# Trips of turned results and probabilities through DRAM: begun by GpSimd instead of SyncE

## The chip, the cores and the metric

The kernel runs on one core of one Trainium2 chip. The metric is device time in microseconds (us), here the median of three runs. The core has five engines with a queue of instructions each: TensorE (PE, with its weight loads as PEld) multiplies matrices, VectorE (DVE) and ScalarE (ACT) work on tiles, GpSimd (POOL) does a few elementwise operations here, and SyncE (SP) only begins DMAs. Each queue is worked off in the order in which the program was written, and an instruction that waits holds all that stand behind it on its engine.

## The reference

One layer of a hybrid encoder, in float32, on 256 tokens of 2048 features:

```python
u   = rmsnorm(h, g_mix)
b_a, c_a, v_a, q, k, v, gl_a, gl_b = split(u @ w_in)
y_a = (b_a * dwconv3(c_a * v_a, conv_w)) @ w_out_a
att = banded_window_attention(rope(q), rope(k), v, sink)      # 16 heads of 64, 4 kv heads
y_b = att @ w_o_attn
h   = h + (sigmoid(gl_a + b) * y_a + sigmoid(gl_b + b) * y_b) @ w_mix_out
up  = dwconv3(rmsnorm(h, g_ffn) @ ffn_w_up) + bias            # 2 x 5632 columns
h   = h + (silu(up[:5632]) * up[5632:]) @ ffn_w_down
out = rmsnorm(h, g_final)
```

## The kernel before, in words

Activations lie transposed on the chip: features on the 128 partitions, the 256 tokens along the row. Every weight is streamed from DRAM once, in chunks of 512 KB (`raw`, five buffers), and each chunk is split into a high part (`whi`, ScalarE, L203) and a low part (`wlo`, VectorE, L214), and so are the activations; three products (high x high, high x low, low x high) then give the precision of the reference.

Most projections are computed in "quads" (L227 to L242): the activations are the stationary operand and four weight tiles, 512 columns, the moving one, three multiplies for each of the two halves of the tokens (L237 to L239). A chunk holds two of the contraction's k-blocks, so it takes 12 multiplies. The result of a quad has tokens on the partitions and has to be turned. VectorE transposes blocks of 32 x 32 out of the two banks (`from_banks`, L329) into a staging tile (`qd`, or `early` in the w_in stage). The blocks then lie in the wrong partitions, and `by_dram` (L306) carries them through DRAM: one DMA writes the whole tile to the DRAM tile `way` (L314), and after it has landed four DMAs read it back, each into 32 partitions (L317), into `qf` (or `early`). Only then do the epilogues of the quad's four tiles read it on VectorE: L512 in the gate and w_up stages, L688 to L698 in the conv branch, L790 and L798 for the two outputs, L807 for w_mix, L886 for w_dn.

The same helper carries two other things. For the first quad of w_in it reads `way` back a second time with rotated blocks for the rotary embedding (L321). And the attention probabilities, transposed by blocks on VectorE (L662, tile `pd`), come back as `pT`, which TensorE reads directly (`att_out`, L676).

The order of the work is written out by hand. `run` (L149) goes through the chunks. For each it emits the fetch of a chunk six ahead (L188, on SyncE), the high part of the chunk three ahead and the low part of the one two ahead, then the multiplies, and then one step of every generator that is under way. A `yield 1` thus means "one chunk later". `by_dram` has one such step between L314 and L317; `quad` has three or four more (`wait`) before the first reader, and lets one (w_up, w_dn) or three quads be under way at a time. That fixes only the order in each engine's queue: an engine that comes early to a reader waits there.

Before the change all of this is begun by SyncE: the weight fetches (L188, L463), the trips (L314, L317, L321), the rotations and copies of the attention (L534, L549), x and most of the output. ScalarE begins three DMAs. GpSimd begins none; it squares and sums for the norms (L420, L422) and scales parts of the output (L943). `wlo` has three buffers, `whi` four, `way` two, `qd` and `qf` one in w_up and w_dn.

Of the kernel before, what the change touches and what calls it, by code (L numbers as in the profile page):

```python
# [53 lines left out]
def hybrid_block_kernel(  # L54
    ctx: ExitStack, tc: tile.TileContext, head, wide, xT, w_q, w_in, w_gate, w_oa, w_o, w_mix, w_up, w_dn, w_end, vec, cst, out
):
    nc = tc.nc
# [9 lines left out]
    x = None  # L67
# [232 lines left out]
    S = 32  # L300
# [5 lines left out]
    def by_dram(dst, src, rot=None):  # L306

        way = turn.tile([4, S, 4, src.shape[-1] // 4], F32, tag="way", name="way")
        nc.sync.dma_start(way.rearrange("a j b x -> (a j) (b x)"), src)  # L314
        yield 1
        for b in range(4):
            nc.sync.dma_start(dst[S * b : S * b + S], way[:, :, b, :].rearrange("a j x -> j a x"))  # L317
        if rot is not None:
            yield 1
            for b in range(4):  # L320
                nc.sync.dma_start(rot[S * b : S * b + S], way[:, :, b ^ 1, :].rearrange("a j x -> j a x"))  # L321

    under_way = [0]

# [10 lines left out]
    def quad(*epis, stage, bufs, wait):  # L335
        def go(banks):
            while under_way[0] >= bufs:
                yield 1
            under_way[0] += 1
            pool = stage()  # L340
            d = pool.tile([P, 4, 2, QUAD * S], F32, tag="qd", name="qd", bufs=bufs)
            yield from from_banks(banks, d)
            f = pool.tile([P, 4, 2, QUAD, S], F32, tag="qf", name="qf", bufs=bufs)
            yield from by_dram(flat_f(f), flat_d(d))

            for _ in range(wait):
                yield 1
            for m, epi in enumerate(epis):
                begin(epi, tile_of(f, m))
                if m < 2:  # L350
                    yield 1
            under_way[0] -= 1

        return go
# [7 lines left out]
    def early_quad(*epis, gap=2):  # L362
        def go(banks):
            while under_way[0] >= 2:
                yield 1
            under_way[0] += 1
            f = early_f[turns_taken[0] % 2]
            turns_taken[0] += 1
            yield from from_banks(banks, early_d)
            yield from by_dram(flat_f(f), flat_d(early_d))  # L370
            for _ in range(4):
                yield 1
            for m, epi in enumerate(epis):
                begin(epi, tile_of(f, m))
                if m < QUAD - 1:
                    for _ in range(gap):
                        yield 1
            under_way[0] -= 1

        return go  # L380
# [200 lines left out]
    def rope_four(banks):  # L581

        while under_way[0]:
            yield 1
        under_way[0] += 2
        f, rot = early_f
        yield from from_banks(banks, early_d)
        yield from by_dram(flat_f(f), flat_d(early_d), flat_f(rot))
        for _ in range(4):
            yield 1  # L590
        for t in (4, 6):
            rcos = rope_buffers()[1]
            for i in range(2):
                m = t - 4 + i
                c, r = by_block_of_tokens(rcos[:, i, :]), tile_of(rot, m)
                nc.vector.tensor_tensor(c, tile_of(f, m), by_block_of_tokens(cs["cos"]), op=ALU.mult)
                nc.vector.tensor_tensor(r, r, by_block_of_tokens(cs["sin"]), op=ALU.mult)
                nc.vector.tensor_tensor(c, c, r, op=ALU.add)
                yield 1
            begin(lambda t=t, rcos=rcos: put_q(t, rcos))  # L600
            if t == 4:
                yield 1
        under_way[0] -= 2
# [479 lines left out]
```

## Time and profile before

| What | Value |
|---|---|
| Median of three runs | 1307.66 us (1307.41 to 1307.69) |
| The profiled execution | 1306.49 us |
| Its span, first to last instruction | 1304.7 us |
| ScalarE busy | 659.4 us, 51% |
| GpSimd busy | 55.4 us, 4% |
| Begun by SyncE: `raw<-in_w_up_dram` | 176 DMAs, 512 KB each, median 4.4 us to landing |
| Begun by SyncE: `way<-qd` | 44 DMAs, 512 KB each, median 2.9 us to landing |
| Begun by SyncE: `qf<-way` | 176 DMAs, 128 KB each, median 2.9 us to landing |
| Queue q1: packets, bytes, share of the 16 DMA engines | 115504, 316.37 MB, 74.0% |

The profile is of one execution; its spans are those of the instructions, and the time of the execution has 1.8 us around them. "busy" counts an engine's own work, not its waits or the issuing of DMAs. A row like `DVE evs L512 <- DMA qf<-way: 3.2, 4, 1.2` reads: VectorE's instruction of line 512 that writes `evs` waited for the landing of the DMA into `qf` from `way`, 3.2 us in total, 4 times, at most 1.2 us. In a timeline the number in brackets is the idle time of the engine before the row, with what ended it. SPq is SyncE's queue.

### The profile page before, as it was taken

How to read it: one execution, taken by the hardware profiler on the slowest of the kernel's cores; microseconds unless marked ns; L12 is line 12 of the kernel's file. 1: busy time of each engine (PE TensorE's matmuls, PEld its weight loads, DVE VectorE, ACT ScalarE, POOL GpSimd, SP SyncE). 2: the span in 40 equal slices, each digit the busy share in tenths (PEclk: the TensorE clock that was granted, in tenths of full speed). 3: DMA queues.
4: the chain of work that ended last, by engine and by line, in shares of the span. 5: the costliest groups of instructions: out<-in, count | busy, mean ns of one | idle time of the engine just before them, and what ended most of it. 6: DMA issues, size and time to landing. Idle time of an engine off the chain costs nothing.

```text
span 1304.7 us, 17038 instructions
## 1 busy us (share of the span) xinstructions
PE 1291.8 (99%) x5918; PEld 1071.3 (82%) x5918; DVE 945.8 (72%) x1403; ACT 659.4 (51%) x927; POOL 55.4 (4%) x66
## 2 busy tenths in 40 slices
PE   9999999999999999999999999999999999999997
PEld 8887777888888888888888888888888888888886
DVE  7879787765656687687798888888888875545454
ACT  7655565454444344445555555555555554434342
POOL 0000000000000000141000000000000000101031
PEclk9999999999999999999999999999999999999999
DMA  8788888778777887776777767676767676767662
GB/s 296 256 264 245 285 267 311 261 243 284 252 257 242 279 289 254 252 242 216 255 247 242 256 213 268 225 257 222 264 224 259 223 259 193 220 200 225 194 210 103
DMA packets 116022, 318.24 MB, mean 244 GB/s; under 512 B 13152, under 2 KB 44768, under 8 KB 115936
## 3 DMA queue, kind: packets, MB, share of 16 engines
q1 hardware_dynamic: 115504, 316.37, 74.0%
q8 instruction: 46, 0.75, 0.2%
q10 hardware_dynamic: 432, 0.79, 0.2%
q14 instruction: 40, 0.33, 0.1%
HBM read 280.15 MB, written 33.55 MB: 240 GB/s over the span
## 4 chain that ended last, share of the span: by engine, by line
PE 93%; DVE 3%; DMA 2%; ACT 1%; issue 1%; SPq 0%; POOLq 0%; DVEq 0%; ACTq 0%
PE pq L239 28%; PE pq L237 28%; PE pq L238 28%; PE ps L261 5%; PE ps L262 3%; DMA raw<-in_w_in_dram 2%; DVE wlo L214 1%; PE av L676 0%; PE warm L445 0%; DMA two<-early 0%; SPq L549 0%; DVE qs L569 0%; ACT whi L203 0%; DVE st L641 0%; DMA pT<-way 0%
## 5 line engine op out<-in xcount | busy, mean ns | idle before, releaser
L214 DVE TENSOR_TENSOR wlo<-raw,whi 128x1024 fp32r<-128x1024 f32 (+3 forms) x465 | 564.3, 1218 | 312.0 <-PE pq L239 159.1
L203 ACT CAST whi<-raw 128x1024 fp32r<-128x1024 f32 (+3 forms) x465 | 482.6, 1040 | 568.4 <-PE pq L238 372.6
L237 PE MATMUL pq<-whi,hs 128*128 128x512 f32 x704 | 274.0, 389 | 0.0
L239 PE MATMUL pq<-wlo,hs 128*128 128x512 f32 x704 | 273.9, 389 | 0.0
L238 PE MATMUL pq<-whi,hs 128*128 128x512 f32 x704 | 273.9, 389 | 0.0
L239 PE MATMUL pq<-wlo,xs 128*128 128x512 f32 x480 | 187.3, 390 | 2.3 <-DVE wlo L214 2.3
L237 PE MATMUL pq<-whi,xs 128*128 128x512 f32 x480 | 187.4, 390 | 0.3 <-ACT whi L203 0.3
L238 PE MATMUL pq<-whi,xs 128*128 128x512 f32 x480 | 186.9, 389 | 0.0
L239 PEld LDWEIGHTS pq<-wlo,hs 128*128 128x128 f32 x704 | 132.1, 188 | 27.6
L237 PEld LDWEIGHTS pq<-whi,hs 128*128 128x128 f32 x704 | 132.1, 188 | 27.4
L238 PEld LDWEIGHTS pq<-whi,hs 128*128 128x128 f32 x704 | 132.1, 188 | 27.3
L239 PEld LDWEIGHTS pq<-wlo,xs 128*128 128x128 f32 x480 | 90.1, 188 | 22.3 <-DVE wlo L214 3.8
L237 PEld LDWEIGHTS pq<-whi,xs 128*128 128x128 f32 x480 | 90.1, 188 | 19.9 <-ACT whi L203 1.5
L238 PEld LDWEIGHTS pq<-whi,xs 128*128 128x128 f32 x480 | 90.1, 188 | 18.5
L329 DVE STREAM_TRANSPOSE qd<-pq 128x512 f32<-128x512 f32 x88 | 62.5, 710 | 5.9 <-PE pq L239 5.0
L237 PE MATMUL pq<-whi,actC 128*128 128x512 f32 x168 | 65.4, 389 | 0.0
L238 PE MATMUL pq<-whi,actC 128*128 128x512 f32 x168 | 65.4, 389 | 0.0
L239 PE MATMUL pq<-wlo,actC 128*128 128x512 f32 x168 | 65.4, 389 | 0.0
L411 ACT ACTIVATE up<-evs,vt 128x256 f32<-128x256 f32 x88 | 50.0, 592 | 0.0
L237 PE MATMUL pq<-whi,ya_att 128*128 128x512 f32 x128 | 49.8, 389 | 0.0
L238 PE MATMUL pq<-whi,ya_att 128*128 128x512 f32 x128 | 49.8, 389 | 0.0
L239 PE MATMUL pq<-wlo,ya_att 128*128 128x512 f32 x128 | 49.8, 389 | 0.0
(178 smaller groups left out, 1515.3 us busy)
## 6 DMA issues: line engine op xcount, KB each, us to landing
raw<-in_w_up_dram SPq DMA_DIRECT2D x176, 512.0 KB, 4.4
raw<-in_w_dn_dram SPq DMA_DIRECT2D x66, 512.0 KB, 4.1
raw<-in_w_gate_dram SPq DMA_DIRECT2D x64, 512.0 KB, 4.4
raw<-in_w_in_dram SPq DMA_DIRECT2D x56, 512.0 KB, 5.9
way<-qd SPq DMA_DIRECT2D x44, 512.0 KB, 2.9
qf<-way SPq DMA_DIRECT2D x176, 128.0 KB, 2.9
raw<-in_w_mix_dram SPq DMA_DIRECT2D x32, 512.0 KB, 4.4
raw<-in_w_end_dram SPq DMA_DIRECT2D x20, 512.0 KB, 4.4
```

The costliest lines, as they stand in the source:

```text
L203: nc.scalar.copy(his[c][:, a:b, :], raws[c](a, b))
L214: nc.vector.tensor_tensor(los[c][:, a:b, :], raw(a, b), his[c][:, a:b, :], op=ALU.subtract)
L237: nc.tensor.matmul(ps, ah, wh, start=k == 0, stop=False)
L238: nc.tensor.matmul(ps, al, wh, start=False, stop=False)
L239: nc.tensor.matmul(ps, ah, wl, start=False, stop=last)
L261: lambda: nc.tensor.matmul(both, hi[:, i, :], moving, start=k == 0, stop=last and turned),
L262: lambda: nc.tensor.matmul(ps[:, 0:T], lo[:, i, :], a[:, 0:T], start=False, stop=last and not turned),
L329: nc.vector.transpose(d[:, :, h, :], ps)
L411: nc.scalar.activation(dst, src, AF.Identity, bias=bias, scale=w1)
```

## The change

All DMAs of `by_dram` are begun by GpSimd's queue. Their shapes, their number, their order among each other and the steps between them stay; everything else that SyncE begins stays there.

```diff
         way = turn.tile([4, S, 4, src.shape[-1] // 4], F32, tag="way", name="way")
-        nc.sync.dma_start(way.rearrange("a j b x -> (a j) (b x)"), src)
+        nc.gpsimd.dma_start(way.rearrange("a j b x -> (a j) (b x)"), src)
         yield 1
         for b in range(4):
-            nc.sync.dma_start(dst[S * b : S * b + S], way[:, :, b, :].rearrange("a j x -> j a x"))
+            nc.gpsimd.dma_start(dst[S * b : S * b + S], way[:, :, b, :].rearrange("a j x -> j a x"))
         if rot is not None:
             yield 1
             for b in range(4):
-                nc.sync.dma_start(rot[S * b : S * b + S], way[:, :, b ^ 1, :].rearrange("a j x -> j a x"))
+                nc.gpsimd.dma_start(rot[S * b : S * b + S], way[:, :, b ^ 1, :].rearrange("a j x -> j a x"))
```

## The prediction

> **What bounds the kernel now.** I read the page first, then the table of busy time by stage, then the waits, and last the order of time in one period of the longest stage. The page (span; busy time, share, instructions):
>
> ```profile
> span 1304.7 us, 17038 instructions
> PE 1291.8 (99%) x5918; PEld 1071.3 (82%) x5918; DVE 945.8 (72%) x1403; ACT 659.4 (51%) x927; POOL 55.4 (4%) x66
> ```
>
> TensorE leaves 12.9 us of the span. The busy times by stretch (columns as in the first row) say where:
>
> ```profile
> core 0: us, PE busy (x) PEld busy (x) DVE busy (x) ACT busy (x) POOL busy (x), PEclk, DMA share, GB/s
> 80.00:160.00 80.00, 77.39 (x363) 61.46 (x361) 67.55 (x132) 46.13 (x101) 0.00 (x0) 1.00 0.86 267
> 232.00:608.00 376.00, 376.00 (x1661) 311.34 (x1660) 254.74 (x322) 174.58 (x210) 27.27 (x31) 1.00 0.78 258
> 608.00:1071.00 463.00, 463.00 (x2044) 383.41 (x2043) 379.07 (x599) 249.46 (x343) 0.00 (x0) 1.00 0.73 243
> 1071.00:1290.00 219.00, 219.00 (x1073) 185.61 (x1073) 116.47 (x124) 92.14 (x103) 25.31 (x29) 1.00 0.65 196
> 1290.00:1304.70 14.70, 5.86 (x48) 5.46 (x46) 7.79 (x22) 2.56 (x8) 2.58 (x2) 0.87 0.38 143
> ```
>
> From 232 to 1290 us TensorE is never idle: nothing that starts earlier there can shorten the kernel. A gain is possible only from 80 to 160 us (2.61 us idle, the attention and w_in stage), since the 8.84 us of the tail hold none of the moved transfers. So the question is mostly the other one: do the trips through DRAM, begun by GpSimd, become late enough to stop TensorE? TensorE is stopped through VectorE: it makes `wlo` (L214), and in its fixed order the readers of a trip's result stand between two `wlo`. Who waits today, in us, times, longest:
>
> ```profile
> DVE evs L512 <- DMA qf<-way: 3.2, 4, 1.2
> ACT whi L203 <- DMA raw<-in_w_in_dram: 21.3, 12, 5.2
> SPq L314 <- DVE qd L329: 172.2, 43, 5.6
> SPq L317 <- DMA way<-pd: 38.8, 7, 7.5
> ```
>
> The first row: readers in w_up hardly wait for a trip. But they have no margin either. One period of w_up in order of time, SyncE's issues first, then VectorE (start, duration; in brackets the idle time before and its cause):
>
> ```profile
> 862.30 0.33 SPq L314 DMA_DIRECT2D way<-qd  x1
> 865.17 1.75 SPq L317 DMA_DIRECT2D qf<-way  x4
> 867.01 11.41 SPq L188 DMA_DIRECT2D raw<-in_w_up_dram  x7
> 884.06 0.33 SPq L314 DMA_DIRECT2D way<-qd  x1
> ...
> 861.57 0.71 DVE L329 STREAM_TRANSPOSE qd<-pq 128x512 f32<-128x512 f32 x1
> 868.68 1.23 DVE L214 TENSOR_TENSOR wlo<-raw,whi 128x1024 fp32r<-128x1024 f32 x1 [1.49 <-PE pq L239]
> 870.29 0.42 DVE L512 TENSOR_TENSOR evs<-qf,r 128x256 f32<-128x256 f32 x1
> 871.40 1.23 DVE L214 TENSOR_TENSOR wlo<-raw,whi 128x1024 fp32r<-128x1024 f32 x1 [0.69 <-PE pq L239]
> 874.12 1.22 DVE L214 TENSOR_TENSOR wlo<-raw,whi 128x1024 fp32r<-128x1024 f32 x1 [1.16 <-ACT up L411]
> 883.96 1.18 DVE L214 TENSOR_TENSOR wlo<-raw,whi 128x1024 fp32r<-128x1024 f32 x1
> ```
>
> The transposed quad goes out at 862.30, is read back from 865.17, and its first reader runs at 870.29. DMA landings (DMA name, count, KB each, median us from issue to landing), first around this trip and then around the next:
>
> ```profile
> way<-qd SPq DMA_DIRECT2D x1, 512.0 KB, 2.8
> qf<-way SPq DMA_DIRECT2D x4, 128.0 KB, 3.9
> ...
> way<-qd SPq DMA_DIRECT2D x1, 512.0 KB, 2.9
> qf<-way SPq DMA_DIRECT2D x4, 128.0 KB, 2.8
> ```
>
> The four read-backs are begun in 1.75 us, 0.44 each, so the fourth near 866.49 (865.17 + 3 x 0.44). With 3.9 us it lands at about 870.4, just where the reader stands. The trip takes its whole margin already.
>
> **The point from which a longer trip costs.** The period is 884.06 - 862.30 = 21.76 us, and it is TensorE's. From the reader to the next `way` VectorE needs 884.06 - 870.29 = 13.77 us, of which 0.69 + 1.16 = 1.85 us are idle and vanish when it runs late: 11.92 us of work. So a trip (issue of `way` to first reader) of up to 21.76 - 11.92 = 9.84 us only eats idle time; what exceeds that makes VectorE's period longer than TensorE's, in every period again. The trips with this short margin are these:
>
> ```profile
> L314 SPq DMA_DIRECT2D way<-qd x14: 326/327/327, 775.3 to 1058.1; - x14
> ```
>
> 14 of 22 in w_up. (The first eight catch up from the start of the stage and have looser readers.) Before the excess reaches TensorE it uses up the head start of `wlo`, once. At its smallest this is 2.8 us: the `wlo` that ends at 883.96 + 1.18 = 885.14 is first used, counting chunks, by this multiply:
>
> ```profile
> 887.92 0.39 PE L239 MATMUL pq<-wlo,hs 128*128 128x512 f32 x1
> ```
>
> **The change, part by part.** It removes 304 issues from SyncE's queue (60 of `way`, 244 read-backs with the four of L321) and puts them, in the same order, on GpSimd's. Waits move with them: the L317 wait for `way` now holds GpSimd. Computation and bytes stay.
>
> *SyncE.* The weight fetches (L188) no longer stand behind a wait for `qd` (172.2 us) or for `way`. In w_up that is worth nothing, TensorE being full. It lets a fetch run beside the trip, though, where SyncE today holds the fetches back until the read-backs are issued (867.01). I price this meeting at half of what the two trips above differ in: (3.9 - 2.8) / 2 = 0.5 us, between 0 and 1.1.
>
> *GpSimd's price for beginning a DMA.* No row shows one. From below it is bounded by SyncE's 0.33 us for `way` (above) and 0.43 for a read-back (min, median, max in ns); from above by what GpSimd needs for one instruction of another kind, its sums (L420: mean 875 ns; then one that ran alone and one that ran beside VectorE):
>
> ```profile
> L317 SPq DMA_DIRECT2D qf<-way x176: 302/426/1804, 275.0 to 1239.2; - x176
> L420 POOL TENSOR_TENSOR sq<-x 128x256 f32<-128x256 f32 x29 | 25.4, 875 | 158.8 <-DVE x L886 108.7 <-DVE x L889 21.9 <-issue 17.0
> 546.25 0.61 POOL L420 TENSOR_TENSOR sq<-x 128x256 f32<-128x256 f32 x1 [2.17 <-DVE x L807]
> 550.87 1.48 POOL L420 TENSOR_TENSOR sq<-x 128x256 f32<-128x256 f32 x1
> ```
>
> The bounds are 0.43 and 1.48 us. I take p = 0.88, the mean of the only instructions of GpSimd that the trace has in number. This is the weakest step.
>
> *The trip in w_up.* `way`: 2.85 - 0.33 + p. Three more read-backs before the last: 3p. The last: the mean of 3.9 and 2.8 is 3.35, so 3.35 - 0.43 + p. Meeting fetches: 0.5. Sum 5.94 + 5p, or 10.34 us at p = 0.88. Excess 10.34 - 9.84 = 0.50 a period, times 14 = 7.0, less the head start of 2.8: **+4.2 us**. Each 0.1 us on p is 7 us on the kernel, and it begins to cost at 9.84 + 2.8 / 14 = 10.04 us, that is p = 0.82.
>
> *The other late stages.* From 232 to 608 us and from 1071 to 1290 us VectorE is idle for 376.00 - 254.74 = 121 and 219.00 - 116.47 = 102 us, and 23 trips that grow by some 2.8 us each use 64 of these 223 us. I book 0. GpSimd's own sums (L420, L422) stand in its queue behind the DMAs and their wait for `way`; but a quad's sums come after its own read-backs anyway. In w_mix a neighbour's trip may delay them by 5p = 4.4 us, and ScalarE's L891 waits for such sums only in w_dn, where the next trip is 22 chunks away. 0, at most 1.
>
> *The w_in stage.* This one has both signs. SyncE, then the two engines that wait:
>
> ```profile
> 127.57 0.42 SPq L314 DMA_DIRECT2D way<-pd  x1
> 128.08 0.58 SPq L188 DMA_DIRECT2D raw<-in_w_in_dram  x1
> 135.43 1.75 SPq L317 DMA_DIRECT2D pT<-way  x4
> 137.28 0.38 SPq L314 DMA_DIRECT2D way<-early  x1
> ...
> 146.17 0.42 DVE L691 TENSOR_TENSOR cvc<-cvc,early 128x256 f32<-128x256 f32 x1 [0.82 <-DMA early<-way]
> 147.89 1.05 ACT L203 CAST whi<-raw 128x1024 fp32r<-128x1024 f32 x1 [3.80 <-DMA raw<-in_w_in_dram]
> ```
>
> From 128.7 to 135.4 no fetch leaves, because SyncE waits for `way`; later ScalarE waits 3.80 us for weights, and this is part of the 2.61 us that TensorE loses. That wait goes. But the two trips still queue behind each other on GpSimd: the first one's read-backs take 4p = 3.5 instead of 1.75 us, the second pays five prices, 5 x 0.88 - 0.33 - 4 x 0.43 = 2.35 us more, and VectorE, which already waits 0.82 us at L691, waits some 4 us longer there. So the late weights are replaced by a late `early`. Bounds -2.6 (all idle recovered) and +6; I take **+1.5 us**, the middle rounded.
>
> *Sum.* The profiled execution took 1306.49 us, 1.17 under the median of the three runs. 1306.49 + 4.2 + 1.5 = 1312.2; on the median, 1307.66 + 5.7 = **1313.4 us**.
>
> **The rivals.** *R1, hidden after all:* p under 0.82, or no meeting with fetches. The trip stays within 9.84 us, w_up costs nothing, w_in gives between -2 and +2: 1307.7 us. For it: the excess is only 0.50 us of 10.34, and a GpSimd whose queue starts DMAs at SyncE's price also ends here. Against it: five prices add up in each trip. The busy shares of the DMA engines from 862.00 us, in 40 slices of 0.225 us, show what SyncE's `way` takes to its first byte:
>
> ```profile
> DMA  0000099999959699896698798958548947899899
> ```
>
> Five empty slices, so 863.1 - 862.3 = 0.8 us. The Trainium skill ("DMA: Bandwidth & Descriptors", section "Latency and other measured facts") gives 0.6 us for a DMA from SyncE and about 1 us for one from GpSimd; by an estimate from that page alone the two DMAs in the chain cost 0.8 us more, the trip would be some 8.8 us, and the time R1's 1307.7; the trace has no DMA from GpSimd to test it.
>
> *R2, faster:* SyncE's release outweighs the rest. The fetches after 128 us leave some 6 us sooner, ScalarE's 3.80 us wait goes, the trips no longer queue behind fetches on SyncE (`way<-pd` waits up to 7.5 us now), and TensorE recovers its 2.6 us or a little more: 1304.7 us. Against it: VectorE's wait at L691 is there today.
>
> *R3, blocked beside VectorE:* GpSimd's sum takes 0.61 us alone and 1.48 us beside VectorE's work. If beginning a DMA suffers likewise, p = 1.48, the trip is 13.34 us, the excess 3.50 x 14 - 2.8 = 46 us, and w_in pays its upper bound: 1360 us. Against it: a sum over 256 columns is other work than beginning a DMA, and the DMAs that VectorE's work runs beside today show no such stretch. The Trainium skill ("SBUF — State Buffer", section "Who interferes with whom") speaks against the change by its advice to begin DMAs elsewhere than on GpSimd when VectorE works beside them, but it limits the blocking to VectorE's two-port modes, and holds two-input operations such as L214 harmless for that; the 1.48 us agrees with its sentence that GpSimd's reads are hit.
>
> **How the numbers follow.** A measurement of this kernel tells 0.2% (2.6 us) from no change. Forecast 0.46, R1 0.34, R2 0.13, R3 0.07. The forecast and R3 are slower by over 0.2%: 0.53. R1 within 0.2%: 0.34. R2 faster: 0.13. The forecast's own range, with p from 0.84 to 1.1, is 1309 to 1330. The range runs from R2's 1304.7, rounded to 1304.5, up to p = 1.1 (trip 11.44, 22.4 - 2.8 = 19.6 us in w_up, 1.5 to 3 in w_in): 1330. R3 and the deeper half of R2 are left out.
>
> **What would show it.** Right: in w_up, `evs` L512 waits for `qf` in nearly every late period, the distance from `way` to `evs` is 10 to 10.7 us, L214's wait for TensorE shrinks, and TensorE waits for `wlo`; the waits of L188 for `qd` and `way` are gone from SyncE. ScalarE's wait for w_in weights falls, and that of L691 or L688 for `early` grows. Wrong: a distance under 9.8 us with TensorE still at 463 of 463 (R1); a TensorE that is shorter idle before 232 us and nothing else (R2); or GpSimd's read-backs further apart than 1.2 us (R3).

## The result

| | Median | Lowest to highest | Runs |
|---|---|---|---|
| before | 1307.54 us | 1306.01 to 1307.69 | 4 |
| after | 1391.13 us | 1387.94 to 1398.87 | 4 |

The change makes the kernel slower: ratio 1.065, 95% interval 1.0623 to 1.0678, or +83.6 us. The forecast was 1313.4 us with a range up to 1330. The profiled execution of after took 1398.87 us, the longest of the four, with a span of 1397.1 us against 1304.7.

The head of the page of after (span; busy time, share, instructions; below, from the part on DMA queues, packets, MB and share of the 16 DMA engines):

```profile
span 1397.1 us, 17166 instructions
PE 1324.2 (95%) x5918; PEld 1080.4 (77%) x5918; DVE 935.3 (67%) x1403; ACT 658.5 (47%) x927; POOL 227.3 (16%) x370
q1 hardware_dynamic: 71728, 252.92, 58.3%
q0 software_dynamic: 20352, 63.46, 15.3%
```

TensorE's idle time has grown from 12.9 to 72.9 us, and its busy time from 1291.8 to 1324.2 us for the same 5918 multiplies. So of the 92.4 us that the span grew by, 60.0 are stalls and 32.4 are multiplies that took longer. The trips now have a DMA queue of their own, q0. (GpSimd's 227.3 us hold its DMA issues, which the page counts there.)

The busy times by stretch show the place. First w_up in before, from its first to its last multiply, then the two attention stretches, w_up and all behind it in after (columns: us; busy time of PE, PEld, DVE, ACT and POOL; granted clock; DMA share; GB/s):

```profile
574.20:1053.30 479.10, 479.10 (x2115) 396.73 (x2114) 389.85 (x606) 257.98 (x351) 10.37 (x13) 1.00 0.72 242
```

```profile
80.00:160.00 80.00, 74.33 (x334) 59.02 (x333) 61.70 (x121) 43.66 (x92) 20.78 (x38) 0.96 0.84 258
160.00:240.00 80.00, 76.22 (x351) 60.10 (x349) 62.52 (x120) 44.00 (x88) 19.59 (x36) 0.96 0.86 258
594.00:1134.00 540.00, 502.15 (x2116) 403.34 (x2115) 385.72 (x606) 256.07 (x349) 74.73 (x124) 0.97 0.70 214
1134.00:1397.00 263.00, 245.13 (x1196) 205.10 (x1194) 140.62 (x169) 104.37 (x125) 42.34 (x51) 0.98 0.63 191
```

w_up begins 594.0 - 574.2 = 19.8 us later, takes 540.0 - 479.1 = 60.9 us more, and what follows it takes 263.1 - 251.4 = 11.7 us more (the rest of either span). TensorE, full in w_up before, is idle there for 540.00 - 502.15 = 37.85 us. In the other 23.05 us TensorE is busy with the same multiplies for longer, at a granted clock of 0.97 instead of 1.00; how far the clock accounts for that is worked out below.

The waits of after (us in total, times, longest) name the chain:

```profile
DVE evs L512 <- DMA qf<-way: 153.3, 29, 10.4
PEld pq L239 <- DVE wlo L214: 73.0, 50, 6.1
PE pq L239 <- DVE wlo L214: 52.5, 36, 5.7
ACT whi L203 <- DMA raw<-in_w_in_dram: 3.0, 3, 1.9
DVE cvc L691 <- DMA early<-way: 10.3, 2, 7.7
```

The wait of `evs` for a read-back was 3.2 us over the whole kernel before; it is 153.3 now, and TensorE waits behind it for `wlo`. One period of w_up, GpSimd's issues first, then SyncE's, then VectorE's; below it the landings of the DMAs begun from 871 to 896 us (count, KB each, median us from issue to landing):

```profile
872.02 0.56 POOL L314 DMA_DIRECT2D way<-qd  x1 [18.76 <-DVE qd L329]
875.77 2.18 POOL L317 DMA_DIRECT2D qf<-way  x4 [3.18 <-DMA way<-qd]
...
896.27 0.56 POOL L314 DMA_DIRECT2D way<-qd  x1 [18.32 <-DVE qd L329]
...
872.86 20.21 SPq L188 DMA_DIRECT2D raw<-in_w_up_dram  x8
...
884.32 0.42 DVE L512 TENSOR_TENSOR evs<-qf,r 128x256 f32<-128x256 f32 x1 [6.61 <-DMA qf<-way]
884.66 1.22 DVE L214 TENSOR_TENSOR wlo<-raw,whi 128x1024 fp32r<-128x1024 f32 x1
```

```profile
raw<-in_w_up_dram SPq DMA_DIRECT2D x8, 512.0 KB, 4.8
way<-qd POOLq DMA_DIRECT2D x1, 512.0 KB, 3.2
qf<-way POOLq DMA_DIRECT2D x4, 128.0 KB, 5.9
```

From `way` to its first reader it is 884.32 - 872.02 = 12.30 us, where the margin was 9.84. VectorE stands idle for 6.61 us in front of L512, with the L214 that TensorE needs behind it. The next `way` goes out at 896.27, so the period is 896.27 - 872.02 = 24.25 us, and the trip plus VectorE's 11.92 us of work is 24.22: VectorE's cycle now sets the pace. The new part is the read-back: 5.9 us from issue to landing instead of 2.8 to 3.9.

What GpSimd needs to begin a DMA (min, median, max in ns) isn't the reason:

```profile
L317 POOL DMA_DIRECT2D qf<-way x176: 550/550/562, 289.4 to 1327.4; - x176
L314 POOL DMA_DIRECT2D way<-qd x44: 558/558/605, 284.3 to 1320.9; - x44
```

### The profile page after: what moved, and what is told of

The parts are those of the page before. It is cut to its first block, busy times and chain, and to the rows that moved or that the text cites. A ratio compares the mean times of both kernels' runs of the same rounds, so it can differ in the third digit from the quotient of the medians.

```text
span 1397.1 us, 17166 instructions
## 1 busy us (share of the span) xinstructions
PE 1324.2 (95%) x5918; PEld 1080.4 (77%) x5918; DVE 935.3 (67%) x1403; ACT 658.5 (47%) x927; POOL 227.3 (16%) x370
## 5 line engine op out<-in xcount | busy, mean ns | idle before, releaser
L214 DVE TENSOR_TENSOR wlo<-raw,whi 128x1024 fp32r<-128x1024 f32 (+3 forms) x465 | 558.1, 1208 | 180.2 <-PE pq L239 113.1
L203 ACT CAST whi<-raw 128x1024 fp32r<-128x1024 f32 (+3 forms) x465 | 477.6, 1035 | 364.9 <-PE pq L238 292.0
L239 PE MATMUL pq<-wlo,hs 128*128 128x512 f32 x704 | 283.2, 402 | 37.9 <-DVE wlo L214 37.8
L237 PE MATMUL pq<-whi,hs 128*128 128x512 f32 x704 | 279.5, 397 | 0.0
L238 PE MATMUL pq<-whi,hs 128*128 128x512 f32 x704 | 279.1, 396 | 0.0
L239 PEld LDWEIGHTS pq<-wlo,hs 128*128 128x128 f32 x704 | 135.4, 192 | 79.9 <-DVE wlo L214 52.0
L238 PEld LDWEIGHTS pq<-whi,hs 128*128 128x128 f32 x704 | 135.1, 192 | 29.1
L237 PEld LDWEIGHTS pq<-whi,hs 128*128 128x128 f32 x704 | 135.3, 192 | 27.5
L512 DVE TENSOR_TENSOR evs<-qf,r 128x256 f32<-128x256 f32 x116 | 46.3, 419 | 153.3 <-DMA qf<-way 153.3
L317 POOL DMA_DIRECT2D qf<-way x176 | 96.0, 552 | 215.9 <-DMA way<-qd 202.5
L314 POOL DMA_DIRECT2D way<-qd x44 | 24.8, 564 | 649.2 <-DVE qd L329 614.2
```

Of the source, the lines that this page charges most:

```text
L203: nc.scalar.copy(his[c][:, a:b, :], raws[c](a, b))
L214: nc.vector.tensor_tensor(los[c][:, a:b, :], raw(a, b), his[c][:, a:b, :], op=ALU.subtract)
L237: nc.tensor.matmul(ps, ah, wh, start=k == 0, stop=False)
L238: nc.tensor.matmul(ps, al, wh, start=False, stop=False)
L239: nc.tensor.matmul(ps, ah, wl, start=False, stop=last)
L314: nc.gpsimd.dma_start(way.rearrange("a j b x -> (a j) (b x)"), src)
```

## The experiments

Three theories for the late read-backs were put against each other. **A**, collision: in SyncE's queue the read-backs stood ahead of the next fetches of weights; now SyncE begins fetches of 512 KB (eight in the 24 us above) while a trip is under way in another queue, and they share the DMA engines. **B**: a read-back begun by GpSimd is slow by itself. **C**: GpSimd's queue gets less of the DMA engines than SyncE's whenever both have work. Landing times below are medians over the late part of w_up; times are medians, ratios are to the kernel before on the same chip.

### Only the write to DRAM on GpSimd

```diff
-        nc.sync.dma_start(way.rearrange("a j b x -> (a j) (b x)"), src)
+        nc.gpsimd.dma_start(way.rearrange("a j b x -> (a j) (b x)"), src)
```

> Only the write into way (L314) is begun by GpSimd; the read-backs stay with SyncE, which so waits for way's landing again and holds the weight fetches back until the read-backs are begun. Theory A (collision: the read-backs are late because the weight fetches, no longer held back, share the DMA engines with them): the last read-back lands 3 to 4 us after it is begun, the trip from way to evs is 8 to 9 us in w_up, TensorE stays full there, 1306 to 1316 us. Theory B (a read-back begun by GpSimd is slow by itself, some 7 us): also 1306 to 1316, since no read-back is GpSimd's. Over 1330 would speak against both and for the write as the cause.

Measured: 1308.8 us, ratio 1.0012 (0.9997 to 1.0026). The landings (w_up, 770 to 1050 us):

```profile
way<-qd POOLq DMA_DIRECT2D x13, 512.0 KB, 2.9
qf<-way SPq DMA_DIRECT2D x52, 128.0 KB, 2.8
```

The write alone costs nothing that shows. The read-backs, in SyncE's queue ahead of the fetches, land as before. What the write costs beside fetches this run doesn't tell: SyncE stands in front of the read-backs until the write has landed, and in the fourteen trips of the table below no fetch is begun between the write's issue and its landing. In after it is 1.9 fetches on average, and there the write isn't spared everywhere: 3.2 us late in w_up, but 4.8 us as the median of all 44, where it was 2.9 us before. Why it is hit less than the read-backs late in w_up stays open.

### Only the read-backs on GpSimd

```diff
-            nc.sync.dma_start(dst[S * b : S * b + S], way[:, :, b, :].rearrange("a j x -> j a x"))
+            nc.gpsimd.dma_start(dst[S * b : S * b + S], way[:, :, b, :].rearrange("a j x -> j a x"))
```

(and the same for `rot`, L321.)

> Only the read-backs (L317, L321) are begun by GpSimd; SyncE begins the write and then goes on to the weight fetches. Theory A: the last read-back lands 6 to 7 us after it is begun, the trip is 11.5 to 13 us in w_up, 1370 to 1395 us. Theory B: the same. Together with the run of the write alone it says which half carries the loss.

Measured: 1349.12 us, ratio 1.0314 (1.0293 to 1.0335): slower, but some 40 us less so than the whole change. Their landing (800 to 1090 us):

```profile
qf<-way POOLq DMA_DIRECT2D x48, 128.0 KB, 7.1
```

The read-backs carry the cost, as expected; the size was expected too large. In this kernel SyncE still waits for `qd` before it begins `way`, and that wait still holds fetches back; that this is the difference wasn't run by itself. The traces show where it lies: here w_up begins no later than before, and its first eight trips cost next to nothing (158.9 us against 157.7); the last fourteen are as late as in the whole change (the first reader 13.4 us after `way`, 12.7 there).

### The whole change, with SyncE held until the read-backs are in

```diff
             nc.gpsimd.dma_start(dst[S * b : S * b + S], way[:, :, b, :].rearrange("a j x -> j a x"))
+        held = turn.tile([1, 8], F32, tag="held", name="held")
+        nc.sync.dma_start(held, dst[S * 3 : S * 3 + 1, 0, 0:8])
```

SyncE copies 32 bytes of the last read-back, and so stands still until it has landed.

> All of the trip is GpSimd's as in the changed kernel, but SyncE is made to stand still: behind the read-backs it has one DMA of 32 bytes that reads the last read-back's result, so that the fetches behind it wait for its landing. Theory A: with the fetches out of the way the last read-back lands 3 to 4.5 us after it is begun, the trip in w_up is 9 to 10.5 us, 1307 to 1330 us. Theory B: the last read-back still takes 6.5 to 7.5 us, the trip stays over 12 us, 1385 us or more (later weights on top).

Measured: 1377.78 us, ratio 1.0529 (1.0504 to 1.0555). The landings (820 to 1110 us), and the wait that is new:

```profile
way<-qd POOLq DMA_DIRECT2D x13, 512.0 KB, 2.9
qf<-way POOLq DMA_DIRECT2D x52, 128.0 KB, 2.8
```

```profile
ACT whi L203 <- DMA raw<-in_w_up_dram: 145.5, 30, 10.8
```

The lateness is gone: with no fetch begun beside them, read-backs begun by GpSimd land in 2.8 us. That speaks against B. The time expected from it was missed, because holding SyncE has a price of its own: it stands still for the whole read-back in every trip, and now the weights are late, by up to 10.8 us in front of ScalarE.

### No weight fetches in w_up, trips on GpSimd and on SyncE

```diff
+    light = set()
...
+                if id(blocks[0][0]) in light:
+                    kept = x[:, 0:4, :].rearrange("p m (h f) -> p (m h) f", f=P)
+                    raws[c] = lambda a, b, kept=kept: kept[:, a:b, :]
+                    return
...
+        if w is w_up:
+            light.update(id(job) for job in jobs)
```

Both kernels leave out the 176 fetches of w_up: its chunks are taken from a tile that lies on the chip already. All else stays, the first kernel with the change, the second without.

> The changed kernel without the weight fetches of w_up: its 176 chunks are made from a tile that is on the chip already, so w_up computes with other numbers and the DMA engines carry hardly anything but the trips there. Theory A: in w_up the last read-back lands 2 to 3.5 us after it is begun, the trip is 8 to 9 us and TensorE is full there, as before. Theory B: the last read-back still takes 6.5 to 7.5 us, the trip over 12 us, and TensorE loses as much in w_up as with the fetches.

> The kernel before, trips by SyncE, without the weight fetches of w_up (they are replaced by a tile on the chip, so w_up computes with other numbers). It gives SyncE's trip with the DMA engines otherwise idle, beside GpSimd's 8.1 us from the run without fetches. Theory A (the price of GpSimd is small, the collision with the fetches is the cause): 7.0 to 7.6 us from way to the last landing, so at most 1 us less than GpSimd's; TensorE full in w_up. Theory B (GpSimd's own price counts): 6 us or less.

Measured, one run each: 1334.68 us with the change, 1304.83 without. Landings and w_up of the first (790 to 1070 us), then landings of the second:

```profile
way<-qd POOLq DMA_DIRECT2D x13, 512.0 KB, 2.9
qf<-way POOLq DMA_DIRECT2D x52, 128.0 KB, 2.9
```

```profile
591.70:1072.90 481.20, 479.50 (x2115) 396.66 (x2114) 395.23 (x611) 259.22 (x353) 74.89 (x126) 1.00 0.15 50
```

```profile
way<-qd SPq DMA_DIRECT2D x13, 512.0 KB, 2.6
qf<-way SPq DMA_DIRECT2D x52, 128.0 KB, 2.9
```

Without fetches beside them the trips on GpSimd cost w_up hardly anything: 479.50 us of work in 481.20. B falls. What is left over the second kernel, some 30 us, is from the other stages, where the fetches remain. The pair also gives GpSimd's own price: with `way` 0.3 us later (2.9 against 2.6) the trip is about 1 us longer in all (the table under the next heading).

### Roles exchanged: fetches on GpSimd, trips on SyncE

```diff
-                nc.sync.dma_start(raw[:, : w.shape[1], :], w)
+                nc.gpsimd.dma_start(raw[:, : w.shape[1], :], w)
```

> The trips stay with SyncE exactly as before; instead the weight fetches (L188) are begun by GpSimd. So SyncE may stand still without holding a fetch. Theory A (the loss comes from fetches that run beside the trip, whoever begins which): the last read-back lands 5.5 to 7.5 us after it is begun in w_up, the trip is 11 us or more, 1350 to 1400 us. Theory C (the trip loses because GpSimd's queue gets less of the DMA engines than SyncE's): the trips, being SyncE's, keep 7.5 us and the kernel 1303 to 1312 us.

Measured: 1367.18 us, ratio 1.0457 (1.0419 to 1.0494). The landings (800 to 1108 us) and one trip:

```profile
way<-qd SPq DMA_DIRECT2D x13, 512.0 KB, 3.1
qf<-way SPq DMA_DIRECT2D x52, 128.0 KB, 6.9
```

```profile
880.45 0.34 SPq L314 DMA_DIRECT2D way<-qd  x1
883.31 1.73 SPq L317 DMA_DIRECT2D qf<-way  x4
...
882.95 0.53 POOL L188 DMA_DIRECT2D raw<-in_w_up_dram  x1 [0.60 <-DVE wlo L214]
885.22 0.53 POOL L188 DMA_DIRECT2D raw<-in_w_up_dram  x1 [1.74 <-DVE wlo L214]
886.36 0.53 POOL L188 DMA_DIRECT2D raw<-in_w_up_dram  x1 [0.61 <-DVE wlo L214]
...
891.59 0.43 DVE L512 TENSOR_TENSOR evs<-qf,r 128x256 f32<-128x256 f32 x1 [5.19 <-DMA qf<-way]
```

Here SyncE begins the trips at its old price, and the read-backs are late all the same: 6.9 us. So it is neither GpSimd (B) nor its queue (C): read-backs in one queue and fetches in another are enough. A holds.

### The whole change, with SyncE held until `way` has landed

```diff
         yield 1
+        held = turn.tile([1, 8], F32, tag="held", name="held")
+        nc.sync.dma_start(held, way[3, S - 1 : S, 3, 0:8])
         for b in range(4):
```

This gives back the wait that SyncE lost, without its place in the order: after the wait the fetches stand in one queue and the read-backs in another.

> The changed kernel, with SyncE made to wait for the landing of way as it did before: a DMA of 32 bytes that reads way stands ahead of the next fetches. The fetches then start together with the read-backs instead of behind them. Theory A in its strict form (what counts is that the read-backs go ahead of the fetches): GpSimd begins four read-backs in 1.6 us and the fetches get in between, the last read-back lands 5 to 7 us after it is begun, 1350 to 1390 us. If standing still for way is enough: 3 to 4 us, trip under 9.5 us, 1307 to 1320 us.

Measured: 1462.59 us, ratio 1.1193 (1.1162 to 1.1225), far worse than expected and than the change itself. The landings (850 to 1190 us) and one trip, SyncE first:

```profile
way<-qd POOLq DMA_DIRECT2D x13, 512.0 KB, 2.9
qf<-way POOLq DMA_DIRECT2D x52, 128.0 KB, 7.9
```

```profile
887.57 0.61 SPq L317 DMA_DIRECT2D held<-way  x1
888.27 17.81 SPq L188 DMA_DIRECT2D raw<-in_w_up_dram  x8
...
887.84 2.19 POOL L319 DMA_DIRECT2D qf<-way  x4 [2.61 <-DMA way<-qd]
```

Of the fetches held back by the wait, three leave together with the read-backs (888.27 to 889.23 us) and a fourth at 891.81, before the last read-back has landed. So it wasn't SyncE's standing still that protected the trips. What protected them was their place in one queue, read-backs first and fetches behind them. (Part of the time is again late weights: ScalarE waits 69.0 us for those of w_up, 30.2 before.)

The number of fetches beside the read-backs isn't what differs. In before, too, one fetch leaves between `way` and its read-backs, in a row that the prediction's timeline leaves out:

```profile
862.72 0.38 SPq L188 DMA_DIRECT2D raw<-in_w_up_dram  x1
```

Between the first read-back's issue and the last one's landing 3.4 more fetches are begun in before and in the kernel with only the write on GpSimd, and 1.9 in after (means of the fourteen trips of the table below). Behind the read-backs in one queue they did them little harm.

### The change in parts

By an argument `queue` of `by_dram`, which stands in place of `nc.sync` in its DMAs, three parts were moved alone (the call shown is that of the later quads): the trips of the w_in stage (`early` and `pd`, 16 of 60), the 44 trips of the later quads (`qd`), and the eight trips of the probabilities (`pd`).

```diff
-    def by_dram(dst, src, rot=None):
+    def by_dram(dst, src, rot=None, queue=nc.sync):
...
-            yield from by_dram(flat_f(f), flat_d(d))
+            yield from by_dram(flat_f(f), flat_d(d), queue=nc.gpsimd)
```

> Only the trips of the w_in stage and the first of the gates (tiles early and pd, 16 of 60) are begun by GpSimd; the 44 of qd stay with SyncE. Theory A: the same collision, trips of 14 to 20 us in w_in, readers of early wait and TensorE loses 15 to 20 us before 240 us; from there on as before: 1322 to 1328 us. The prediction's step for this stage said +1.5 us: 1309.

> The other part: only the 44 trips of qd (gates from the second quad on, w_oa, w_o, w_mix, w_up, w_dn) are begun by GpSimd; early and pd stay with SyncE. Theory A (a fetch that runs beside the read-backs makes them late, in every stage): TensorE as before up to 240 us, trips of 12 to 13 us in w_up; with the part of w_in alone at +11 us and the whole at +84, 1375 to 1385 us. Much under 1370 would mean that the parts feed each other.

> Only the eight trips of the probabilities (pd to pT) are begun by GpSimd. SyncE no longer stands still for way<-pd, up to 7.5 us at a time, so the w_in weights come earlier. Theory A: the pT read-backs land 2 to 4 us later than before; TensorE reads pT itself and had 2 to 6 us of margin, so 1306 to 1315 us. If the freed SyncE outweighs it (the prediction's second rival, in the only place where it could): 1303 to 1306 us.

Measured: w_in stage 1319.5 us, ratio 1.0091 (1.0076 to 1.0106); later quads 1373.2 us, 1.0487 (1.046 to 1.0514); probabilities 1306.86 us, 0.999 (0.998 to 1.0). The first two, 11.2 and 65.3 us over the kernel before on their chips, both a little under what was expected, make 76.5 of the 83.6 us. Of the w_in kernel one wait, of the probabilities' kernel the landing of the read-backs from 80 to 235 us:

```profile
DVE cvc L691 <- DMA early<-way: 14.4, 2, 7.7
```

```profile
pT<-way POOLq DMA_DIRECT2D x32, 128.0 KB, 5.8
```

The read-backs of `pT` land in 5.8 us instead of 2.9, as late as the others, and cost nothing: their readers come late enough. So it isn't the lateness that has the price but the lateness beyond the margin of its reader. That the 11.2 us of the w_in stage are therefore the trips of `early` is concluded, not run by itself.

### SyncE's wait in the attention taken away without a second queue

The wait for `way<-pd` that the prediction wanted to remove can also be removed by reading the probabilities back one step later, all on SyncE. This starts from before:

```diff
-    def by_dram(dst, src, rot=None):
+    def by_dram(dst, src, rot=None, late=0):
...
-        yield 1
+        for _ in range(1 + late):
+            yield 1
...
-        yield from by_dram(f.rearrange("p a e n k i -> p a (e n k i)"), d.rearrange("p b e n k i -> p (b e n k i)"))
+        yield from by_dram(f.rearrange("p a e n k i -> p a (e n k i)"), d.rearrange("p b e n k i -> p (b e n k i)"), late=1)
```

> The kernel before, all trips with SyncE, but the read-backs of the probabilities are begun one chunk later (two steps instead of one between L314 and L317). SyncE then stands still less for way<-pd, and the read-backs still go ahead of the fetches behind them. Theory A: what was lost from 140 to 160 us to late weights comes back in part: 1304.5 to 1307 us, against 1307.5. No change beyond 0.15% would leave it open.

Measured: 1304.35 us (1302.52 to 1305.77) against 1307.86, ratio 0.9969 (0.9957 to 0.9981): a small gain, but one that the interval sets apart from no change. SyncE's queue at the place that the prediction showed, then the wait for weights:

```profile
128.24 0.42 SPq L314 DMA_DIRECT2D way<-pd  x1
...
129.24 0.81 SPq L314 DMA_DIRECT2D way<-early  x1
130.15 0.72 SPq L188 DMA_DIRECT2D raw<-in_w_in_dram  x1
135.26 1.75 SPq L318 DMA_DIRECT2D pT<-way  x4
```

```profile
ACT whi L203 <- DMA raw<-in_w_in_dram: 11.3, 5, 4.3
```

Another trip and a fetch now leave between 128.7 and 135.3 us, where SyncE only waited before, and ScalarE's wait for weights falls from 21.3 to 11.3 us. That this is where the 3.5 us were won isn't shown: TensorE stands idle for 1.83 us from 80 to 160 us here and for 2.61 before, but for 1.71 in the kernel without fetches and with SyncE's trips, where this stage is unchanged.

## Why the prediction was wrong

It had the direction and the mechanism, and failed in one term of the sum, the meeting of trips and fetches. Two terms were wrong in opposite directions, the price p too high and the meeting too low; with the right p and the meeting as booked the sum would have given no loss in w_up. So it was in part luck that the direction came out.

The table sets the forecast's trip in w_up beside the measured trips up to their last landing, as means over the fourteen trips ahead of the last of w_up (begun from 752.4 to 1036.4 us in before; the same trips in the others), worked out from each DMA's issue and landing in the trace (us):

| Part of the trip | forecast | before | after | after, no fetches | before, no fetches |
|---|---|---|---|---|---|
| `way`, issue to landing | 3.40 | 2.89 | 3.58 | 2.99 | 2.61 |
| landing to first read-back's issue | 0 | 0.02 | 0.57 | 0.57 | 0.08 |
| three more issues | 2.64 | 1.32 | 1.63 | 1.63 | 1.30 |
| last read-back, issue to landing | 3.80 | 3.52 | 6.77 | 2.91 | 3.18 |
| meeting with fetches | 0.5 | in the rows | in the rows | none | none |
| **sum** | **10.34** | **7.74** | **12.55** | **8.10** | **7.17** |

**The point from which a trip costs** (9.84 us; period = trip + 11.92) held: the period of after is 24.25 us, and the sum gives 24.22. That VectorE's idle time in the period goes first, and who waits next, `evs` and then TensorE for `wlo`, came as said.

**The price p** was taken at 0.88 us from GpSimd's sums; it is 0.55, 550/550/562 ns, even beside VectorE. A sum was the wrong kind of row: SyncE's 0.43 us for the same DMA was the nearer end. With p = 0.55 the forecast's own formula gives 5.94 + 2.75 = 8.69 us, inside the margin, and so R1. The kernel without fetches shows that world: trips of 8.10 us and a nearly full TensorE in w_up. The other extra of GpSimd, 0.57 us from a landing to the issue that waited for it, was missing from the sum; its whole own price is 8.10 - 7.17 = 0.93 us a trip. The Trainium skill ("DMA: Bandwidth & Descriptors", section "Latency and other measured facts") had 0.4 us more to the first byte; the 0.38 us on `way` agree, but that rule's conclusion, R1, did not come, since it says nothing of the neighbour.

**The meeting with fetches** was put at 0.5 us, bounds 0 and 1.1. It is 12.55 - 8.10 = 4.45 us; before, it was 7.74 - 7.17 = 0.57. This is the step that failed. The two trips from which it was priced differed by 1.1 us while the read-backs stood ahead of the fetches; they couldn't show what happens when that order is gone. The prediction saw that a fetch would run beside the trip, and then took the price from trips whose fetches stood behind the read-backs in one queue. The unpriced resource was the place in the queue. The Trainium skill ("DMA: Bandwidth & Descriptors", section "Issuing engines are not separate DMA queues") holds that all DMAs share 16 DMA engines whoever begins them, and that more beginners only save issue time. The first half agrees with the read-backs of 5.9 us; the second leaves out what these runs show, that a second queue can cost as much as 6.5% here. The Trainium skill's section "Queues, rings and completion order" (the same page) has each DMA engine take turns between its queues, packet by packet; an estimate by it, half the engine and so about twice 2.9 us, agrees with the 5.8 to 6.3 us of `pT` and of after, and falls short of the 6.9 and 7.1 us of the kernels with the roles exchanged and with only the read-backs moved, and of the 7.9 us of the burst.

**From the excess to the time.** By the forecast's formula a trip of 12.30 us costs 14 x (12.30 - 9.84) - 2.8 = 31.6 us. This step held for the trips to which it was applied: from the first to the last of the fourteen with the short margin, `way` to `way`, after takes 319.7 us and before 282.9, 36.8 us more, with trips of 12.7 us on average; and each of these thirteen periods is its trip plus 11.9 us, whether or not TensorE's clock was low in it. What the sum left out are the first eight trips of w_up, which the prediction called looser. From `way` to the first reader they take some 13 to 15.7 us where it was 8.6 to 10.1, and their periods take 181.5 us instead of 157.7: another 23.8 us. In the kernel with the change and without fetches the same periods take 160.0 us, so here too it is the meeting.

TensorE's 23.05 us of longer multiplies in w_up had no step in the prediction either. The trace's clock records have seven pieces at half speed there, of 3.4 or 6.8 us, 30.7 us in all, so at most half of that, 15.4 us, is the clock's; the rest stays open. As VectorE's cycle sets the pace in the late periods, the slower multiplies fill time there in which TensorE would have stood idle; no run shows that they lengthen the kernel. The Trainium skill ("TensorE: Matmul & The Clock Gate", Part 1) describes such a fall to half speed after an idle window of about 3.4 us. The length of the pieces agrees; the stalls before them are shorter, since in the 3.4 us ahead of each piece TensorE was idle for only 1.9 to 3.2 us.

**The other late stages**, booked at 0, at most 1, are longer by 11.7 us after w_up, and the stages before w_up by 19.8 us. The kernel with only the w_in trips moved reaches the first trip of w_up 9.2 us later than before, and it takes 4.1 us more from the last trip to the end, where it moved nothing; so not all of this can be put down to the late trips. VectorE's idle sum (223 us) was no cover: a wait of 5 us in front of one reader, as I read it, falls on the few chunks behind that reader and is not spread over the stage. No run takes these stages by themselves.

**The w_in stage** was put at +1.5 us, bounds -2.6 and +6; it is +11.2 in the kernel that moved these trips alone. Both signs came as named: ScalarE's wait for w_in weights fell from 21.3 to 3.0 us, and the wait at L691 grew from 0.82 to 7.7. Only the second was far larger; the traces fit the same collision.

**The rivals.** R2's release of SyncE seems to exist: a part of it, taken alone by the later read-back, gives 1304.35 us where R2 said 1304.7. That the numbers lie so near is partly luck, since that kernel gives back only some of SyncE's waits. In this change the collision buries it. R3 falls: a read-back costs GpSimd 550 to 562 ns with VectorE busy for 67% of the span, while its place in the time, 1360 us, was nearer than the forecast for another reason. The page "SBUF — State Buffer" ("Who interferes with whom") of the Trainium skill, which holds two-input operations harmless for a DMA's beginning, agrees with these rows.

## What to carry to other kernels

A wait at the head of a DMA queue can be an order worth keeping: if small transfers that someone waits for share DMA engines with a bulk prefetch, keep them in one queue with the small ones ahead, and move the wait (here by reading back one step later) rather than the queue. Before you move a DMA to a second queue, ask which transfers were behind it in the first, price the trip as if these ran beside it, and compare it with the margin of its reader. Do so for every trip of a stage, and not only for those with the shortest margin.

## What the runs showed of the hardware that was not expected

- Read-backs are slowed by fetches of another queue, whichever engine begins which: the same read-back of 128 KB takes 2.8 to 2.9 us (medians) alone or ahead in its queue, 5.8 to 7.1 beside fetches from the other queue, and 7.9 when the fetches start together with it.
- Short stalls are enough for TensorE's clock to fall. In w_up of after each of the seven pieces at half speed follows a stretch of 3.4 us in which TensorE was idle for 1.9 to 3.2 us. But not every longer multiply is the clock's: with SyncE held until the read-backs were in, TensorE was idle for 17.65 us in w_up at a clock of 1.00, and its busy time, 487.65 us, was still 8.55 more than before. Why stays open.

```profile
608.40:1113.70 505.30, 487.65 (x2114) 395.85 (x2115) 385.39 (x602) 251.49 (x350) 73.96 (x124) 1.00 0.65 230
```

- The read-backs are cut otherwise when GpSimd begins them. DMA packets in a part of w_up, before (770 to 1050 us) and after (800 to 1130):

```profile
DMA packets 24151, 67.69 MB, mean 242 GB/s; under 512 B 2674, under 2 KB 9330, under 8 KB 24132
```

```profile
DMA packets 19976, 70.46 MB, mean 214 GB/s; under 512 B 2815, under 2 KB 2815, under 8 KB 19957
```

Before, 9330 - 2674 = 6656 packets lie between 512 B and 2 KB, just 52 read-backs of 128 packets of 1 KB; after there are none. The larger packets brought no speed that shows: 2.9 us on either engine without fetches.
